# Seven Strassen products for the FFN's output projections, with operands combined by the input projections

## The chip, the cores and the metric

One core of a Trainium2 chip runs the kernel; everything is float32. The metric is the device time of one execution in microseconds. The kernel before was timed three times: 2273.18, 2268.51 and 2273.02, median 2273.02. The engines are named as in the profile: PE is the matrix engine (PEld its loading of the stationary operand), DVE the vector engine, ACT the scalar engine, POOL the third elementwise engine, SP the queue from which most transfers are issued.

## The reference

One layer of a streaming encoder on 1024 tokens of width 1024, hidden width 2816:

```python
x = x + 0.5 * swiglu_ffn(rms_norm(x, ffn1_norm), ffn1_w_in, ffn1_w_out)
u = rms_norm(x, mix_norm)
# one input projection of u; band attention A, differential attention B; gates
x = x + (g_a * (y_a @ w_branch_a) + g_b * (y_b @ w_branch_b)) @ w_o
x = x + 0.5 * swiglu_ffn(rms_norm(x, ffn2_norm), ffn2_w_in, ffn2_w_out)
return rms_norm(x, final_norm)

def swiglu_ffn(x, w_in, w_out):
    gate, up = jnp.split(x @ w_in, 2, axis=-1)
    return (silu(gate) * up) @ w_out
```

The change concerns the product with `w_out` in both FFNs: 1024 x 2816 times 2816 x 1024.

## The kernel before

**Precision.** Every float32 operand of a matmul is split into a rounded part and the remainder: `split` casts on ACT (line 95, `whi`) and subtracts on DVE (line 100, `wlo`). `mm3` (lines 124 to 128) then issues three matmuls: high x high, high x low, low x high.

**Input projections** (`ffn_in`, and the mixer's in the same way) already use seven products in place of eight, in the Winograd form of Strassen's method. `norm_pair` normalises token tile pr and token tile pr + 4 together, transposes them through PE (line 184) and stores the seven combinations `A11, A12, S1, S2, S3, S4, A22` as split pairs in fourteen buffers of the ring `big`. `weight_ops` makes `T1, T2, T3, N4` from four weight blocks, and `PRODUCTS` names the three PSUM chains q, r and s in which products are summed. For each of 22 column blocks j the seven products take 84 matmuls; the last of them is held back and issued after the first product of the next j (`later`, `flush`). The sinks apply SiLU, multiply, and store the hidden block h[j] (128 hidden channels x 1024 tokens) to device memory in two halves (line 330).

**Output projections** (`ffn_out`) are plain. The residual rows (eight tiles of 128 tokens) stay in SBUF. The hidden blocks are taken in 11 groups of two j. For a group, each hidden block and its weight rows are loaded (512 KB each) and split; then for each token tile t and each half dh of the output columns, six matmuls of 128x512 go into one bank `po`, and DVE adds half of it to the residual (line 361). In the last group the token tiles go in the order 4, 0, 5, 1, 6, 2, 7, 3, and `finish` is called behind each. In the first FFN the sums of the group before the last go to device memory and back (`x_part`), and `finish1` stores the new residual and calls `norm_pair` as soon as tiles t and t + 4 are there; `next(mix)` starts the mixer's first column block after pair 3. In the second FFN `finish2` normalises a tile and stores it. A first column block of any input projection is done in two pieces of 256 tokens, of which the first needs only pairs 0 and 1.

**Order and buffers.** The program is traced as straight code. A planner with a simulated timeline puts the instructions of each engine into a fixed order when the program is built; where an instruction is ready earlier in that simulation, it is moved ahead. At run time each engine and each queue works its list strictly in order and waits on semaphores. Buffers come from rings: `raw` (six of 4 KB for each partition), `w` (split units, 2 KB), `f` (temporaries, 2 KB), `t` (three), `big` (fourteen of 8 KB). PSUM has eight banks, six in the ring `mm` and two in `tr`.

Of the kernel before, what the change touches and what calls it, by code (L numbers as in the profile page):

```python
# [16 lines left out]
P = 128  # L17
S = 1024
# [5 lines left out]
NF = FF // P  # L24
A_HEADS, A_DIM = 8, 64
# [18 lines left out]
RAW, WU, TF, TT = 6, 20, 8, 3  # L44
# [8 lines left out]
def hybrid_layer_kernel(ctx, tc, x, ffn1_norm, ffn1_w_in, ffn1_w_out, mix_norm, w_mix_in,  # L53
# [85 lines left out]

    def rstd_row(xt):  # L140

        ssq = small.tile([P, 2], F32, tag="ssq", name="ssq")
        for d in range(2):
            nc.scalar.activation(out=junk, in_=xt[:, d * HALF:(d + 1) * HALF], func=AF.Square,
                                 scale=D ** -0.5, accum_out=ssq[:, d:d + 1])
# [20 lines left out]
    def norm_pair(pr, xt, gain, u, ps, on_vector=False):  # L166

        diag = []
        for h in range(2):
# [4 lines left out]
            for d in range(2):  # L174
                c = slice(d * HALF, (d + 1) * HALF)
                (nc.vector if on_vector else nc.gpsimd).tensor_tensor(
                    out=xt[h][:, c], in0=xt[h][:, c], in1=gain[:, c], op=ALU.mult)
        c = slice(pr * P, (pr + 1) * P)

        def block(h, d):  # L180

            tr = ps.tile([P, 4, P], F32, tag="tr", bufs=2, name="tr")
            for k in range(4):
                nc.tensor.matmul(tr[:, k, :], xt[h][:, d * HALF + k * P:d * HALF + (k + 1) * P], diag[h],  # L184
                                 start=True, stop=True)
# [125 lines left out]
    def ffn_in(w_in, u, ps, h_d, extra=None):  # L311

        silu = []
        for j in range(NF):
# [3 lines left out]
            def make_sink(c0, n, j=j):  # L318
                keep = {}

                def sink(th, blk, ap):
# [13 lines left out]
    def ffn_out(w_out, h_d, x_src, x_part, ps, finish):  # L335


        xu = [big([P, 2, D], "x", F32) for _ in range(NT // 2)]
        xs = [xu[t // 2][:, t % 2, :] for t in range(NT)]
        for t in range(NT):  # L340
            nc.scalar.dma_start(out=xs[t], in_=x_src[t])
        groups = [range(j, j + 2) for j in range(0, NF, 2)]
        for g, js in enumerate(groups):
            last = g == len(groups) - 1
            hs, ws = [], []
            for j in js:
                hr = load(h_d[j], raw_tile([P, S]))
                wr = load(w_out[j * P:(j + 1) * P, :], raw_tile([P, D]))
                hs.append([split_units(hr[:, c * HALF:(c + 1) * HALF]) for c in range(2)])
                ws.append([split_units(wr[:, c * HALF:(c + 1) * HALF]) for c in range(2)])  # L350
            for t in ([4, 0, 5, 1, 6, 2, 7, 3] if last else range(NT)):
                xt = xs[t]
                if last and x_part:
                    xt = load(x_part[t], raw_tile([P, D], "xt"))
# [517 lines left out]
```

## Time and profile before

| what | before |
|---|---|
| median of three runs | 2273.02 us |
| the profiled execution | 2272.47 us |
| its span, first to last instruction | 2270.7 us |
| busy: PE, DVE, ACT, POOL | 2160.4, 1450.3, 916.4, 286.8 us |
| mean granted clock of PE | 0.979 |
| first output projection, first to last matmul | 463 to 716 us |
| second output projection, first to last matmul | 2015 to 2261 us |

The stages in order: the first input projection to 463 us, the first output projection, the mixer's input projections and attention, the merge up to about 1600 us, the second input projection, the second output projection. A busy engine's matmuls overlap, so a matmul's listed duration is longer than its spacing. Idle time before an instruction is put down to what released it last.

### The profile page before, as it was taken

What the parts mean: (1) busy time and instruction counts of PE and PEld (TensorE: products, weight loads), DVE (VectorE), ACT (ScalarE), POOL (GpSimd) and SP (SyncE); (2) the same over time, 40 slices, a digit from 0 to 9 for tenths busy, and PEclk for the clock granted to TensorE, in tenths of its full rate; (3) what the DMA queues carried; (4) which work ended last, traced back from release to release, by engine and by line L of the source; (5) the groups of instructions that cost most, each with busy time, mean ns of one, the idle gap of its engine ahead of it and who ended that gap; (6) DMA issues with size and microseconds to landing.
All of it is one profiled execution on the core that took longest, in us unless ns stands there. A gap on an engine that the chain in (4) does not pass through costs nothing. (4 is left out here: it accounts for less than half of the span.)

```text
span 2270.7 us, 29665 instructions
## 1 busy us (share of the span) xinstructions
PE 2160.4 (95%) x10637; PEld 1827.8 (80%) x10637; DVE 1450.3 (64%) x2608; ACT 916.4 (40%) x1840; POOL 286.8 (13%) x371
## 2 busy tenths in 40 slices
PE   5999999999998899999999988899899999999998
PEld 4888888888887898888878877778788888888886
DVE  8655555566677756654378877658655555557677
ACT  5433333322124544444388755245433333322213
POOL 6021000000005100000066223004200000000000
PEclk8999999999999999999999998999899999999999
DMA  4364222433226454442596465654322222253331
GB/s 142 93 165 112 84 84 82 139 126 101 92 86 238 140 167 167 167 144 89 137 220 158 128 173 146 209 179 153 95 82 84 83 80 87 78 174 102 96 100 75
DMA packets 228611, 287.20 MB, mean 126 GB/s; under 512 B 13820, under 2 KB 160268, under 8 KB 228464
## 3 DMA queue, kind: packets, MB, share of 16 engines
q1 hardware_dynamic: 221952, 269.00, 38.9%
q0 software_dynamic: 4064, 7.39, 1.6%
q10 hardware_dynamic: 2448, 8.91, 1.1%
q8 instruction: 84, 1.38, 0.3%
q14 instruction: 63, 0.52, 0.1%
HBM read 202.14 MB, written 83.10 MB: 126 GB/s over the span
## 5 line engine op out<-in xcount | busy, mean ns | idle before, releaser
L95 ACT CAST whi<-raw 128x512 fp32r<-128x512 f32 x376 | 228.4, 622 | 664.8 <-PE po L127 321.2
L100 DVE TENSOR_TENSOR wlo<-raw,whi 128x512 fp32r<-128x512 f32 x373 | 257.1, 702 | 115.1 <-ACT whi L95 78.1
L361 DVE SCALAR_TENSOR_TENSOR x<-po,x 128x512 f32<-128x512 f32 x336 | 223.5, 687 | 119.7 <-PE po L128 119.6
L128 PE MATMUL po<-whi,wlo 128*128 128x512 f32 x704 | 273.6, 389 | 0.0
L127 PE MATMUL po<-wlo,whi 128*128 128x512 f32 x704 | 273.5, 389 | 0.0
L126 PE MATMUL po<-whi 128*128 128x512 f32 x704 | 259.6, 389 | 1.0 <-ACT whi L95 1.0
L111 DVE TENSOR_TENSOR c<-prod,c 128x512 f32<-128x512 f32 (+1 forms) x201 | 133.3, 665 | 178.9 <-PE prod L128 174.9
L100 DVE TENSOR_TENSOR wlo<-T,whi 128x512 fp32r<-128x512 f32 x189 | 134.3, 710 | 151.7 <-ACT whi L95 120.0
L95 ACT CAST whi<-T 128x512 fp32r<-128x512 f32 x192 | 120.0, 625 | 236.1 <-PE prod L127 201.2
L137 POOL TENSOR_TENSOR r<-v,neg_half 128x1 f32<-128x1 f32 x64 | 43.0, 673 | 1333.9 <-DVE v L147 1295.9
L126 PEld LDWEIGHTS po<-whi 128*128 128x128 f32 x704 | 132.0, 188 | 29.5 <-ACT whi L95 1.8
L128 PEld LDWEIGHTS po<-whi,wlo 128*128 128x128 f32 x704 | 132.1, 188 | 27.4
L127 PEld LDWEIGHTS po<-wlo,whi 128*128 128x128 f32 x704 | 132.2, 188 | 27.3
L184 PE MATMUL tr<-dg,xt 128*128 128x128 f32 x384 | 63.9, 329 | 53.2 <-DVE A22l L100 17.4
L100 DVE TENSOR_TENSOR wlo<-N,whi 128x512 fp32r<-128x512 f32 x61 | 42.2, 692 | 103.6 <-ACT whi L95 80.8
L250 ACT COPY c<-prod 128x512 f32<-128x512 f32 (+1 forms) x201 | 104.2, 574 | 5.9 <-PE prod L128 3.2
L184 PEld LDWEIGHTS tr<-dg,xt 128*128 128x128 f32 x384 | 59.2, 238 | 57.9 <-issue 25.7
L594 ACT ACTIVATE pm<-pm,mn 128x640 f32<-128x640 f32 (+7 forms) x128 | 94.1, 736 | 16.8 <-DVE mn L592 15.5
L126 PE MATMUL prod<-A11h,whi 128*128 128x512 f32 (+1 forms) x252 | 97.0, 385 | 0.9 <-ACT A11h L95 0.7
L128 PE MATMUL prod<-S1h,wlo 128*128 128x512 f32 (+1 forms) x252 | 96.1, 381 | 0.9 <-DVE wlo L100 0.9
L592 DVE CUSTOM_DVE_ANT_0 pm<-sc,nb 128x640 f32<-128x640 f32 (+7 forms) x128 | 88.1, 698 | 13.7 <-PE sc L585 10.8
L126 PE MATMUL prod<-S1h,whi 128*128 128x512 f32 (+1 forms) x252 | 96.2, 382 | 0.6 <-ACT S1h L95 0.6
(229 smaller groups left out, 5483.9 us busy)
## 6 DMA issues: line engine op xcount, KB each, us to landing
raw<-in_ffn_w_in_dram SPq DMA_DIRECT2D x88, 512.0 KB, 3.9
raw<-h SPq DMA_DIRECT2D x44, 512.0 KB, 4.0
raw<-in_ffn_w_out_dram SPq DMA_DIRECT2D x44, 512.0 KB, 4.2
h<-c SPq DMA_DIRECT2D x84, 256.0 KB, 2.0
raw<-in_w_mix_in_dram SPq DMA_DIRECT2D x40, 512.0 KB, 4.2
wr<-in_w_o_dram SPq DMA_DIRECT2D x40, 256.0 KB, 2.8
v<-vo SPq DMA_DIRECT2D x32, 256.0 KB, 2.3
qs<-q SPq DMA_DIRECT2D x16, 512.0 KB, 9.6
```

The lines of the kernel that those rows point to most:

```text
L95: nc.scalar.copy(out=hi, in_=src)
L100: (nc.gpsimd if on_pool else nc.vector).tensor_tensor(out=lo, in0=src, in1=h, op=ALU.subtract)
L111: nc.vector.tensor_tensor(out=out_, in0=a, in1=b, op=op)
L126: nc.tensor.matmul(ps, a[0], b[0], start=first, stop=False, skip_group_check=shared)
L127: nc.tensor.matmul(ps, a[0], b[1], start=False, stop=False, skip_group_check=shared)
L128: nc.tensor.matmul(ps, a[1], b[0], start=False, stop=last, skip_group_check=shared)
L137: nc.gpsimd.tensor_tensor(out=r, in0=v, in1=neg_half, op=ALU.pow)
L184: nc.tensor.matmul(tr[:, k, :], xt[h][:, d * HALF + k * P:d * HALF + (k + 1) * P], diag[h], start=True, stop=True)
L250: nc.scalar.copy(out=self.held[name], in_=p)
L361: nc.vector.scalar_tensor_tensor(out=xt[:, c], in0=po, scalar=0.5, in1=xt[:, c], op0=ALU.mult, op1=ALU.add)
L592: nc.vector.tensor_tensor_reduce(out=d3, in0=sc, in1=nb.rearrange("p (n w) -> p n w", n=n), scale=1.0, scalar=3e38, op0=ALU.add, op1=ALU.m ...
L594: nc.scalar.activation(out=dst, in_=dst, func=AF.Exp, bias=mn, scale=-1.0, accum_out=rs)
```

## The change

The output projections are done in seven products as well. The hidden matrix is divided into four: token halves (tiles 0 to 3, tiles 4 to 7) by even and odd hidden blocks; the weight matrix into even and odd hidden blocks by column halves. Each product m runs over the full contraction of one quadrant: 11 steps i, in each of which one operand block (128 channels x 512 tokens) and one weight block (128 x 512) meet, four token tiles of three matmuls each, summed in four PSUM banks over all 11 steps. The chain q holds four banks from product 0 to 6 and is read in passing after products 0, 2, 4 and 6; r (products 1 and 3) and s (product 5) share the other four. A reading adds half the banks to one quadrant of the residual.

The input projection now keeps the hidden blocks of an even and an odd j, and `hidden` forms S1, S3, S2, S4 from them on DVE and stores seven blocks for each pair of j, in place of the four halves. The weight differences are made in place in the loaded blocks, and the loads of weight blocks are placed by the table `BLOCK_LOADS`. The residual is held in halves: tokens 0 to 3 in two buffers of `big`, tiles 4 to 7 in `raw` and `f`. Quadrant (0,1) is complete after product 3, (1,1) after 4, (0,0) after 5, (1,0) after 6. The first two token groups are stored as they are complete; for the first FFN they are loaded again for `norm_pair`, which runs for all four pairs behind product 6 (`late1`), with `next(mix)` after pair 1. For the second FFN, tiles 0 to 3 are finished after product 5 (`early2`), tiles 4 to 7 at the end (`late2`). The round trip through `x_part` in the first FFN is gone. The rings change from 20 to 18 units and from 8 to 10 temporaries.

```diff
+NK = NF // 2
...
-RAW, WU, TF, TT = 6, 20, 8, 3
+RAW, WU, TF, TT = 6, 18, 10, 3
...
+    def halves(xt):
+        return [xt[:, :HALF], xt[:, HALF:]]
+    def store_rows(dst, xt):
+        for d in range(2):
+            nc.sync.dma_start(out=dst[:, d * HALF:(d + 1) * HALF], in_=xt[d])
...
                 c = slice(d * HALF, (d + 1) * HALF)
                 (nc.vector if on_vector else nc.gpsimd).tensor_tensor(
-                    out=xt[h][:, c], in0=xt[h][:, c], in1=gain[:, c], op=ALU.mult)
+                    out=xt[h][d], in0=xt[h][d], in1=gain[:, c], op=ALU.mult)
...
-    def ffn_in(w_in, u, ps, h_d, extra=None):
...
+        silu, hid = [], {}
+        def put(name, i, src):
+            nc.sync.dma_start(out=h_ops[name][i], in_=src)
+        def hidden(j, th):
+            i, odd = j // 2, j % 2
+            if (th, odd) != (1, 0):
+                put(("A11", "A22" if th else "A12")[odd], i, hid[j, th])
+            if not (odd and th):
+                return
+            a11, a21, a12, a22 = (hid.pop(k) for k in ((j - 1, 0), (j - 1, 1), (j, 0), (j, 1)))
+            s1, s2 = temp([P, HALF], "hs1"), temp([P, HALF], "hs2")
+            add(s1, a21, a22)
+            put("S1", i, s1)
+            add(a21, a11, a21, ALU.subtract)
+            put("S3", i, a21)
+            add(s2, s1, a11, ALU.subtract)
+            put("S2", i, s2)
+            add(a12, a12, s2, ALU.subtract)
+            put("S4", i, a12)
...
                     keep[th, blk] = ap
                     if (th, 0) in keep and (th, 1) in keep:
                         h = keep[th, 1]
-                        nc.vector.tensor_tensor(out=h, in0=h, in1=keep[th, 0], op=ALU.mult)
-                        nc.sync.dma_start(out=h_d[j][:, th * HALF + c0:th * HALF + c0 + n], in_=h)
+                        if n == HALF:
+                            hid[j, th] = h
+                        elif (j, th) not in hid:
+                            hid[j, th] = temp([P, HALF], "hid")
+                        nc.vector.tensor_tensor(out=h if n == HALF else hid[j, th][:, c0:c0 + n], in0=h,
+                                                in1=keep[th, 0], op=ALU.mult)
+                        if c0 + n == HALF:
+                            hidden(j, th)
                 return sink
             yield from strassen_t(weights(w_in, j * P, FF + j * P, () if j else SPARE),
                                   u, ps, make_sink, 1 if j else 2)
-    def ffn_out(w_out, h_d, x_src, x_part, ps, finish):
...
+    OUT_PRODUCTS = (("A11", "B11", "q", 0, 0, False), ("S1", "T1", "r", 1, 1, False),
+                    ("S2", "T2", "q", 0, 1, False), ("S4", "B22", "r", 0, 1, True),
+                    ("S3", "T3", "q", 1, 1, True), ("A12", "B21", "s", 0, 0, True),
+                    ("A22", "N4", "q", 1, 0, True))
...
+    BLOCK_LOADS = {(0, 0): (("B11", 0, 8),), (0, 1): (("B11", 8, 11), ("B12", 0, 4)),
+                   (0, 3): (("B12", 4, 8),), (0, 7): (("B12", 8, 11),),
+                   (1, 0): (("B22", 0, 4),), (1, 4): (("B22", 4, 8),), (1, 8): (("B22", 8, 11),),
+                   (3, 0): (("B21", 0, 4),), (3, 4): (("B21", 4, 8),), (3, 8): (("B21", 8, 11),)}
...
+    def ffn_out(w_out, x_src, x_dst, ps, early, late):
...
+        wv = w_out.rearrange("(i two p) d -> two p i d", two=2, p=P)
+        blocks, banks, begun = {}, {}, set()
+        rows = [[[None, None] for _ in range(4)] for _ in range(2)]
+        def load_block(name, i0, i1):
+            n = 2 if name == "B11" else 4
+            for j0 in range(i0, i1, n):
+                r = min(n, i1 - j0)
+                b = raw_tile([P, 2, HALF], name) if n == 2 else big([P, 4, HALF], name, F32)
+                nc.sync.dma_start(out=b[:, :r], in_=wv[int(name[1]) - 1][
+                    :, j0:j0 + r, (int(name[2]) - 1) * HALF:int(name[2]) * HALF])
+                for i in range(r):
+                    blocks[name, j0 + i] = b[:, i, :]
+        def weight(name, i):
+            if name in ("T1", "T2"):
+                t = blocks["B11", i]
+                add(t, blocks["B12" if name == "T1" else "B22", i], t, ALU.subtract)
+            elif name == "T3":
+                t = blocks["B12", i]
+                add(t, blocks["B22", i], t, ALU.subtract)
+            else:
+                t = blocks["B21" if name == "N4" else name, i]
+            return t
+        def prepare(th, dh):
+            for t in range(4):
+                if th == 0:
+                    if t % 2 == 0 and rows[0][t][1 - dh] is None:
+                        xu = big([P, 2, 2, HALF], "x", F32)
+                        for n in range(4):
+                            rows[0][t + n // 2][n % 2] = xu[:, n // 2, n % 2, :]
+                elif dh:
+                    rows[1][t][1] = temp([P, HALF], "xc")
+                elif t % 2 == 0:
+                    xu = raw_tile([P, 2, HALF], "xc")
+                    rows[1][t][0], rows[1][t + 1][0] = xu[:, 0, :], xu[:, 1, :]
+        for m, (an, bn, chain, th, dh, done) in enumerate(OUT_PRODUCTS):
+            first = chain not in banks
+            c = slice(dh * HALF, (dh + 1) * HALF)
+            if first:
+                banks[chain] = [ps.tile([P, HALF], F32, tag=tag, bufs=n, name="po") for tag, n in
+                                (("mm", 6), ("mm", 6)) + ((("mm", 6),) * 2 if chain == "q" else (("tr", 2),) * 2)]
+            for i in range(NK):
+                if (m, i) in BLOCK_LOADS:
+                    for args in BLOCK_LOADS[m, i]:
+                        load_block(*args)
+                if m:
+                    ha = temp([P, HALF], "ha")
+                else:
+                    if i % 4 == 0:
+                        h4 = big([P, 4, HALF], "ha", F32)
+                    ha = h4[:, i % 4, :]
+                a = split_units(load(h_ops[an][i], ha))
+                w = split_units(weight(bn, i))
+                if bn == "B21":
+                    n4 = blocks["B21", i]
+                    add(n4, n4, blocks["B11", i], ALU.subtract)
+                for t in range(4):
+                    mm3(banks[chain][t], [v[:, t * P:(t + 1) * P] for v in a], w,
+                        first and i == 0, i == NK - 1, not first)
+                if m == 0 and i == 0:
+                    flush()
+                if i == 5 and (th, dh) not in begun:
+                    begun.add((th, dh))
+                    prepare(th, dh)
+                    for t in range(4):
+                        load(x_src[4 * th + t][:, c], rows[th][t][dh])
+            for t in range(4):
+                xt = rows[th][t][dh]
+                nc.vector.scalar_tensor_tensor(out=xt, in0=banks[chain][t], scalar=0.5, in1=xt,
+                                               op0=ALU.mult, op1=ALU.add)
+                if done and not th:
+                    nc.sync.dma_start(out=x_dst[t][:, c], in_=xt)
+            if m == 5:
+                early()
+        late(rows[1])
...
-    h_d = drams(NF, [P, S], "h")
+    h_ops = {n: drams(NK, [P, HALF], f"h{n}") for n in U_OPS}
...
-        def finish1(t, xt):
-            if not u2:
-                u2.update(new_u())
-            nc.sync.dma_start(out=x_mid[t], in_=xt)
-            pair[t // 4] = xt
-            if t < 4:
-                norm_pair(t, [pair[0], pair[1]], gain, u2, ps)
-                if t == 3:
+        def late1(rows1):
+            for t, xt in enumerate(rows1):
+                store_rows(x_mid[4 + t], xt)
+            u2.update(new_u())
+            for t, xt in enumerate(rows1):
+                norm_pair(t, [halves(load(x_mid[t], raw_tile([P, D], "xt"))), xt], gain, u2, ps)
+                if t == 1:
                     next(mix)
...
-        ffn_out(ffn1_w_out[0], h_d, rows(x), x_part, ps, finish1)
+        ffn_out(ffn1_w_out[0], rows(x), x_mid, ps, lambda: None, late1)
...
         run_all(ffn2)
-        flush()
...
-        ffn_out(ffn2_w_out[0], h_d, x_mix, None, ps, finish2)
+        def early2():
+            for t in range(4):
+                finish2(t, halves(load(x_part[t], raw_tile([P, D], "xt"))))
+        def late2(rows1):
+            for t, xt in enumerate(rows1):
+                finish2(4 + t, xt)
+        ffn_out(ffn2_w_out[0], x_mix, x_part, ps, early2, late2)
```

More of the change, by code (lines that the diff above doesn't have):

```diff
@@ L143, in rstd_row @@
         for d in range(2):
-            nc.scalar.activation(out=junk, in_=xt[:, d * HALF:(d + 1) * HALF], func=AF.Square,
+            nc.scalar.activation(out=junk, in_=xt[d], func=AF.Square,
                                  scale=D ** -0.5, accum_out=ssq[:, d:d + 1])
@@ L183, in block @@
             for k in range(4):
-                nc.tensor.matmul(tr[:, k, :], xt[h][:, d * HALF + k * P:d * HALF + (k + 1) * P], diag[h],
+                nc.tensor.matmul(tr[:, k, :], xt[h][d][:, k * P:(k + 1) * P], diag[h],
                                  start=True, stop=True)
@@ L333, in ffn_in @@
                                   u, ps, make_sink, 1 if j else 2)
-    def ffn_out(w_out, h_d, x_src, x_part, ps, finish):
[L338 to L354, printed above, removed]
-                tc_ = slice((t % 4) * P, (t % 4 + 1) * P)
-                for dh in range(2):
-                    c = slice(dh * HALF, (dh + 1) * HALF)
-                    po = ps.tile([P, HALF], F32, tag="mm", bufs=6, name="po")
-                    for n in range(len(js)):
-                        mm3(po, [v[:, tc_] for v in hs[n][t // 4]], ws[n][dh], n == 0, n == len(js) - 1)
-                    nc.vector.scalar_tensor_tensor(out=xt[:, c], in0=po, scalar=0.5, in1=xt[:, c],
-                                                   op0=ALU.mult, op1=ALU.add)
-                if last:
-                    finish(t, xt)
-                elif x_part and g == len(groups) - 2:
-                    nc.sync.dma_start(out=x_part[t], in_=xt)
@@ L452, in hybrid_layer_kernel @@
                 gain = load_gain(ffn1_norm[0], nc.scalar)
-            norm_pair(pr, xt, gain, u, ps, pr == 0)
+            norm_pair(pr, [halves(v) for v in xt], gain, u, ps, pr == 0)
             if pr == 1:
@@ L803, in hybrid_layer_kernel @@
         u3 = {}
[L804 removed]
+        ffn2 = ffn_in(ffn2_w_in[0], u3, ps)
         for g in range(2):
@@ L823, in hybrid_layer_kernel @@
                                     u3.update(new_u())
-                                norm_pair(t, [xt[t], xt[t + 4]], gain, u3, ps)
+                                norm_pair(t, [halves(xt[t]), halves(xt[t + 4])], gain, u3, ps)
                                 if t == 3:
@@ L837, in finish2 @@
                 c = slice(d * HALF, (d + 1) * HALF)
-                nc.vector.scalar_tensor_tensor(out=o[:, c], in0=xt[:, c], scalar=r, in1=gain_f[:, c],
+                nc.vector.scalar_tensor_tensor(out=o[:, c], in0=xt[d], scalar=r, in1=gain_f[:, c],
                                                op0=ALU.mult, op1=ALU.mult)
                 nc.sync.dma_start(out=out[t * P:(t + 1) * P, c], in_=o[:, c])
-        ffn_out(ffn2_w_out[0], h_d, x_mix, None, ps, finish2)
+        def early2():
[5 more added lines that the diff above has]
+        ffn_out(ffn2_w_out[0], x_mix, x_part, ps, early2, late2)
 _INS = ['x', 'ffn1_norm', 'ffn1_w_in', 'ffn1_w_out', 'mix_norm', 'w_mix_in', 'b_gate', 'rel_bias_a',
```

7 lines of the change are left out of this document (2 added, 5 removed).

## The prediction

> **What bounds the kernel now.** I read the page first, then busy times in chosen stretches, then the groups of the first output projection alone, and last the chain and the order of time at the seams. From the page:
>
> ```profile
> span 2270.7 us, 29665 instructions
> PE 2160.4 (95%) x10637; PEld 1827.8 (80%) x10637; DVE 1450.3 (64%) x2608; ACT 916.4 (40%) x1840; POOL 286.8 (13%) x371
> L361 DVE SCALAR_TENSOR_TENSOR x<-po,x 128x512 f32<-128x512 f32 x336 | 223.5, 687 | 119.7 <-PE po L128 119.6
> L128 PE MATMUL po<-whi,wlo 128*128 128x512 f32 x704 | 273.6, 389 | 0.0
> L127 PE MATMUL po<-wlo,whi 128*128 128x512 f32 x704 | 273.5, 389 | 0.0
> L126 PE MATMUL po<-whi 128*128 128x512 f32 x704 | 259.6, 389 | 1.0 <-ACT whi L95 1.0
> ```
>
> TensorE is the busy engine, and the 3 x 704 = 2112 matmuls into `po` are the two output projections (1056 each). Their 389 ns overlap one another, so the price of one is their spacing, from the chain of waits, where each second group of 96 matmuls begins with this piece (start us, us, what):
>
> ```profile
> 2155.18 0.68 PE po L126 x3
> 2176.94 0.68 PE po L126 x3
> ```
>
> 21.76 us for 96 matmuls (2 j x 8 t x 2 dh x 3) is **0.2267 us a matmul**. Busy times by stretch (columns: length, then busy us of PE, PEld, DVE, ACT, POOL with instructions, granted clock, DMA share, GB/s):
>
> ```profile
> 250.00:440.00 190.00, 190.00 (x840) 157.30 (x839) 102.82 (x160) 68.41 (x120) 0.00 (x0) 1.00 0.26 84
> 490.00:690.00 200.00, 200.00 (x884) 165.62 (x883) 139.94 (x220) 42.15 (x72) 0.00 (x0) 1.00 0.31 100
> 716.00:760.00 44.00, 30.07 (x178) 27.09 (x177) 43.48 (x60) 26.14 (x52) 30.01 (x24) 0.81 0.44 141
> ```
>
> The first is the inside of an input projection, the second the inside of an output projection: PE has no idle time in either, at full clock, so a matmul taken out there is 0.2267 us off the end. The third is the passage from the first output projection to the mixer: there DVE is busy 43.48 of 44 us and PE waits for the normalisation.
>
> **The change part by part.** *Matmuls.* Before: 11 groups x 96 = 1056 for each projection. After: 7 products x 11 steps x 4 token tiles x 3 = 924, of the same shape (128x512 moving, 128 columns stationary), three in a row into one bank as now. 132 fewer, twice: 264 x 0.2267 = **-59.8 us**. A step (12 matmuls) then lasts 2.72 us.
>
> *What feeds a step.* Durations from the groups of the output projection alone, and from the whole run for the weight difference:
>
> ```profile
> L361 DVE SCALAR_TENSOR_TENSOR x<-po,x 128x512 f32<-128x512 f32 x148 | 98.7, 687 | 53.1 <-PE po L128 53.1
> L100 DVE TENSOR_TENSOR wlo<-raw,whi 128x512 fp32r<-128x512 f32 x72 | 47.1, 684 | 7.5 <-PE po L127 7.5
> L95 ACT CAST whi<-raw 128x512 fp32r<-128x512 f32 x72 | 42.1, 621 | 153.7 <-PE po L127 152.2
> L111 DVE TENSOR_TENSOR T<-raw 128x512 f32<-128x512 f32 x128 | 90.0, 703 | 3.9 <-DMA raw<-in_ffn_w_in_dram 2.4
> ```
>
> Splits rise from 88 to 154 for each projection (an operand and a weight block in every one of 77 steps). Weight differences are new: T1, T2, T3, N4, 11 of each, 44 DVE adds. The additions out of PSUM fall from 176 to 28, since a chain is read once after 11 steps. DVE: before 88 x 0.684 + 176 x 0.687 = 181 us of 239; after 154 x 0.684 + 44 x 0.703 + 28 x 0.687 = 155 us of 924 x 0.2267 = 209, 74%. The tightest steps (products with a difference) need 2 x 0.684 + 0.703 = 2.07 us plus 0.25 for the reads, of 2.72. ACT needs 2 x 0.621 = 1.24. So PE stays the bound, and the feed costs **0**. Its cover is the ring of units: the ACT row shows that the casts wait for PE to release units (152.2 of 153.7 us), so they run as early as the ring lets them. A ring of 18 holds 4.5 steps of four units, 12 us ahead of PE, against 0.62 + 0.68 = 1.3 us for cast and remainder. Without that cover it is 1.3 x 154 = 200 us. The ring for temporaries, 8 to 10, keeps six for operands once four hold residual halves: six steps, 16 us. I take nothing for either.
>
> *Input projection.* Each pair of j gains four DVE adds and writes seven blocks of 256 KB instead of four. 88 adds x 0.703 = 62 us over both; per 190 us (ten j) that is 14 us on DVE's 102.8, 61%, beside PE's matmuls at 100%. The transfers gain 0.79 MB per 38 us, 21 GB/s on 84. **0**; it would cost the 62 us if DVE had been the bound. The stores wait on DVE in SP's queue, with weight loads behind them; three j of raw buffers (six tiles, two each) cover that. From the DMA issues, the sequencer's own row, and the transfer rate between 440 and 480 us (each figure a 40th of it):
>
> ```profile
> h<-c SPq DMA_DIRECT2D x84, 256.0 KB, 2.0
> raw<-h SPq DMA_DIRECT2D x44, 512.0 KB, 4.0
> L117 SPq DMA_DIRECT2D raw<-h x44: 319/319/338, 399.9 to 2199.3; - x44
> GB/s 168 348 377 365 393 336 332 414 172 0 102 258 426 348 279 270 313 424 369 107 139 176 395 88 0 106 279 139 0 0 141 121 0 0 0 16 147 213 361 57
> ```
>
> *Transfers of the output projection.* 77 operand blocks (20 MB), 11.5 MB of weights, the residual rows 4 MB, now all in SP's queue: about 125 issues x 0.32 = 40 us of SP in 209, and 170 GB/s, where this row holds 332 to 414 for 6 us. The dense place is the start: in product 0's 30 us come 11 operand blocks, B11, B12 and a quarter of the rows, 2.9 + 2.9 + 2.9 + 1 = 9.7 MB. The large buffers are released from product 0 of the last j on, 16 us (six products of 2.72) before, so 46 us x 350 GB/s = 16 MB are to be had. If all had to be issued behind the stores of the last hidden block, those wait for the flushed product and its five DVE operations (2.7 + 3.5 us), and 1.75 MB of B11 and B12 (5 us) with about 1 us of split follow: 12 us for each projection. Bounds 0 and +24, I take **+2**, because PE shows no idle time at the same seam now (the row from 250 and the one from 490 frame it, and the chain has nothing there).
>
> *The passage to the mixer.* Before, the last group interleaves token tiles so that pair 0 is normalised under matmuls. After, the half (1,0) comes out of product 6 for all four pairs at the end, and the four pairs follow it. The rows around it, before (order of time), then the groups of 716 to 760, then three DVE instructions in a row and two short matmuls in a row:
>
> ```profile
> 715.71 0.39 PE L128 MATMUL po<-whi,wlo 128*128 128x512 f32 x1
> L184 PE MATMUL tr<-dg,xt 128*128 128x128 f32 x112 | 20.2, 344 | 10.9 <-DVE s L111 6.5 <-DVE A22l L100 3.1 <-ACT a L193 1.3
> L100 DVE TENSOR_TENSOR wlo<-T,whi 128x512 fp32r<-128x512 f32 x4 | 3.8, 953 | 0.0
> L176 POOL TENSOR_TENSOR xt<-xt,gain 128x512 f32<-128x512 f32 x10 | 12.9, 1324 | 0.6 <-ACT junk L144 0.6
> 743.73 0.68 DVE L100 TENSOR_TENSOR A11l<-tr,A11h 128x512 fp32r<-128x512 f32 x1
> 744.33 0.67 DVE L111 TENSOR_TENSOR s<-s,tr 128x512 f32<-128x512 f32 x1
> 744.92 0.68 DVE L111 TENSOR_TENSOR s<-tr,a 128x512 f32<-128x512 f32 x1
> 756.19 0.28 PE L126 MATMUL prod<-A11h,whi 128*128 128x256 f32 x1
> 756.31 0.28 PE L127 MATMUL prod<-A11l,whi 128*128 128x256 f32 x1
> ```
>
> Of 178 matmul records in these 44 us, 112 are transposes, 66 products of 256 columns at 0.12 us, 8 us of the mixer's work: 36 us are lost. After: DVE runs 4 reads and 4 pairs x 13 instructions (4 sums, 5 remainders, 2 diagonals, 2 small) = 56, at 43.48 / 60 = 0.725 us each 41 us, and about 4 us pass first: store of the half (2.0), because the gain overwrites it, gain (1.3), transposes and a copy. The gains and sums of the rows that are complete earlier, and the mixer's first weights, lie in product 6, where DVE is free for 12 of 30 us. Set against 45 us: the first half-width piece needs only pairs 0 and 1, 84 x 0.12 = 10 us, and A11 and S1 of the second piece another 3. Lost 32 us: **-4**. Bounds: at DVE's 0.60 spacing, 34 + 4 - 13 = 25, so -11; at the pace of the kernel's start, where four pairs also come one behind the other (below), 50 + 4 - 13 = 41, +5, and +8 with the mixer's first weights late too.
>
> ```profile
> 13.04 4.57 PE L184 MATMUL tr<-dg,xt 128*128 128x128 f32 x24 [13.04 <-DVE dg L172]
> 62.59 1.13 PE L184 MATMUL tr<-dg,xt 128*128 128x128 f32 x8 [0.88 <-DVE A22l L100]
> ```
>
> *The end.* Before:
>
> ```profile
> 2252.38 2.73 DVE L838 SCALAR_TENSOR_TENSOR o<-x,r,gain 128x512 f32<-128x512 f32 x4
> 2260.87 0.39 PE L128 MATMUL po<-whi,wlo 128*128 128x512 f32 x1
> 2265.89 1.41 DVE L838 SCALAR_TENSOR_TENSOR o<-x,r,gain 128x512 f32<-128x512 f32 x2 [0.73 <-POOL r L137]
> ```
>
> From the last matmul's end (2261.3) to the span's 2270.7 are 9.4 us, of which 3.4 follow the last output row. After, tiles 0 to 3 finish under product 6; behind the last matmul stand a read, the sum, the root and the rest of eight output halves at 0.66 us, about 7.5 us, and 3.4: **+1.5** (-1 to +4).
>
> **Sum**: -59.8 + 2 - 4 + 1.5 = -60.3 from the profiled execution's 2272.5, and 0.5 to the median: **2213 us**, its own range 2201 to 2225.
>
> **Rivals.** *Seams starve*: operands come late at the starts of both projections, +24 less the 2 counted: **2235**. For it: the stores and loads share SP's queue. Against: no such gap now.
>
> *DVE becomes the bound* in products with a difference. At the 0.953 us that a remainder took beside POOL in the passage, a step needs 3 x 0.953 + 0.25 = 3.1 us, 0.4 over, in 44 steps of each projection, 35 us: **2248**. Against: POOL is at 0.00 inside projections.
>
> *Transfers in series, slower than before.* If one waits for the one before it, products 0 and 1 (60 us of PE) need 22 operand blocks at 2.0, six tiles of B11 at 4.0, six of 1 MB (B12, B22) at 8.0 and eight half rows at 2.0: 132 us. Less 60 and the 16 us of lead, 56 us late in each projection: 2213 + 112 = **2325**. It ends behind the kernel of before from 30 us of lateness in each. Against it stands the rate row: 512 KB in 4.0 us is 131 GB/s, and the row holds 332 to 414, so several are under way at once.
>
> [...]
>
> *Not Strassen in effect* (PE's spacing gets worse with chains of 11 steps): each matmul has the shape and the order of now, and I see no row for it.
>
> **Chances.** Likeliest 0.69; starving seams 0.16; DVE the bound 0.08; series 0.05; the rest 0.02. A measurement of this kernel can't tell less than about 0.2% (4.5 us) from no change. Faster 0.93, same 0.02, slower 0.05: only the series and part of the rest end above. The range 2196 to 2238 takes in the passage's lower bound (-11, with the end's -1 and no seam: 2201, and 5 us for ten temporaries in the later stages) and the starving seams, and leaves the last three out.
>
> **What would show it.** Right: 1848 matmuls into `po`, 0.2267 us apart with PE at 100% inside both projections; DVE at some 74% there; 28 + 28 reads of PSUM; from the last `po` matmul of the first projection to a full PE some 45 us, with 256-column products in it from about 20 us on. Wrong: idle PE released by a DMA of `ha` or of weights early in a projection, by `wlo` or `T` at every step, or a passage over 50 us.

## The result, and the profile after

The changed kernel takes 2210.61 us (median of four runs, 2207.22 to 2211.25), the kernel before 2270.77 us (four runs, one more than ahead of the prediction, 2266.45 to 2273.18). The ratio is 0.9734 with a 95% interval of 0.9714 to 0.9754: 60 us faster. The prediction was 2213.

From the page of the changed kernel (busy time of each engine, then groups):

```profile
span 2209.0 us, 29778 instructions
...
PE 2100.4 (95%) x10373; PEld 1779.8 (81%) x10373; DVE 1448.2 (66%) x2620; ACT 991.2 (45%) x1972; POOL 286.4 (13%) x371
...
L128 PE MATMUL po<-wlo,whi 128*128 128x512 f32 x616 | 240.0, 390 | 0.0
...
L101 DVE TENSOR_TENSOR wlo<-B,whi 128x512 fp32r<-128x512 f32 x154 | 107.0, 695 | 129.2 <-ACT whi L96 129.2
L96 ACT CAST whi<-B 128x512 fp32r<-128x512 f32 x154 | 95.7, 622 | 206.9 <-PE po L128 185.3
```

PE has 60.0 us less busy time and the same share. 3 x 616 = 1848 matmuls go into `po`, 264 fewer. DVE does 296 additions out of PSUM fewer and 308 other instructions more (132 splits, 88 weight differences, 88 sums of hidden blocks), and its busy time stays where it was (1450.3 us before, 1448.2 now). ACT's grows by 75 us. The casts of weights still wait for PE to release units (185.3 of 206.9 us), as before.

Busy times by stretch of the changed kernel (length, then PE, PEld, DVE, ACT, POOL with instructions, granted clock, DMA share, GB/s):

```profile
250.00:440.00 190.00, 190.00 (x840) 157.43 (x839) 115.06 (x180) 69.41 (x120) 0.00 (x0) 1.00 0.32 104
457.20:686.20 229.00, 228.71 (x1008) 188.84 (x1006) 156.68 (x250) 97.67 (x175) 7.46 (x6) 1.00 0.53 173
480.00:500.00 20.00, 20.00 (x90) 16.58 (x89) 19.25 (x33) 5.68 (x10) 0.00 (x0) 1.00 0.84 298
500.00:520.00 20.00, 20.00 (x90) 16.58 (x89) 19.21 (x32) 9.78 (x17) 0.00 (x0) 1.00 0.74 255
520.00:600.00 80.00, 80.00 (x355) 66.28 (x354) 46.63 (x74) 34.16 (x60) 0.00 (x0) 1.00 0.36 107
686.20:734.90 48.70, 33.69 (x214) 31.48 (x213) 39.23 (x58) 27.55 (x62) 30.48 (x28) 0.82 0.32 101
710.00:715.00 5.00, 5.00 (x27) 5.00 (x27) 4.74 (x8) 2.08 (x4) 2.84 (x3) 0.54 0.13 44
715.00:720.00 5.00, 5.00 (x45) 5.00 (x44) 2.31 (x4) 1.04 (x3) 1.30 (x1) 1.00 0.36 105
```

Inside the input projection (first row) and the output projection (second) PE has as good as no idle time. The first output projection's stretch also holds 84 matmuls of the input projection's end: 924 + 84 = 1008. The two rows from 480 are to be remembered: DVE is busy 19.2 of 20 us there, against 46.63 of 80 behind them. The row from 686.20 is the passage to the mixer; PE does 128 transposes and 86 half-width products in its 48.7 us.

Where the 61.7 us between the two spans lie can be read from four landmarks of each kernel, the tile views of `po` and of the gates `sig` (duration min/median/max, first to last start). Before:

```profile
L128 PE MATMUL po<-whi,wlo x352: 389/389/476, 463.6 to 715.7; 128*128 128x512 f32 x176
L520 ACT ACTIVATE sig<-prod,bg x8: 682/687/690, 1018.7 to 1141.7; 128x512 f32<-128x512 f32 x8
L128 PE MATMUL po<-whi,m0l x128: 387/389/476, 1480.6 to 1575.7; 128*128 128x512 f32 x128
L128 PE MATMUL po<-whi,wlo x352: 388/389/389, 2010.5 to 2260.9; 128*128 128x512 f32 x176
```

After:

```profile
L129 PE MATMUL po<-whi,wlo x308: 388/390/390, 457.4 to 685.8; 128*128 128x512 f32 x154
L622 ACT ACTIVATE sig<-prod,bg x8: 682/682/687, 991.5 to 1114.2; 128x512 f32<-128x512 f32 x8
L129 PE MATMUL po<-whi,m0l x128: 388/390/477, 1450.3 to 1543.2; 128*128 128x512 f32 x128
L129 PE MATMUL po<-whi,wlo x308: 388/390/390, 1968.6 to 2197.0; 128*128 128x512 f32 x154
```

| stretch | before | after | difference | forecast |
|---|---|---|---|---|
| start to the last matmul of the first output projection | 715.7 | 685.8 | -29.9 | -29.9 + 1 |
| from there to the first gate (passage and mixer) | 303.0 | 305.7 | +2.7 | -4 |
| first to last gate | 123.0 | 122.7 | -0.3 | 0 |
| last gate to last matmul of the merge (attention) | 434.0 | 429.0 | -5.0 | 0 |
| from there to the last matmul of the second output projection | 685.2 | 653.8 | -31.4 | -29.9 + 1 |
| from there to the end | 9.8 | 12.0 | +2.2 | +1.5 |

So the total is right while two of its parts are not: the passage is 6.7 us worse than forecast, and 5.0 us come from the attention, where nothing was forecast. Both figures come again in other kernels: in the three of the experiments below that change neither the rings nor the passage (`cut_p5`, `dve_extra`, `dma_extra`) passage and mixer take 305.0 to 305.7 us and the attention 428.3 to 428.8.

The passage in order of time, changed kernel (start us, us, instruction, idle time before it and what ended it), PE:

```profile
685.81 0.39 PE L129 MATMUL po<-whi,wlo 128*128 128x512 f32 x1
692.23 3.79 PE L192 MATMUL tr<-dg,xc 128*128 128x128 f32 x16 [6.03 <-DVE dg L180]
...
705.99 0.38 PE L127 MATMUL prod<-A11h,whi 128*128 128x256 f32 x1 [0.68 <-ACT A11h L96]
708.57 0.58 PE L127 MATMUL prod<-S1h,whi 128*128 128x256 f32 x1 [2.19 <-ACT S1h L96]
...
733.98 1.13 PE L192 MATMUL tr<-dg,xt 128*128 128x128 f32 x8 [1.38 <-DVE A22l L101]
734.86 0.36 PE L127 MATMUL prod<-A11h,whi 128*128 128x256 f32 x1
```

The same stretch on POOL and ACT:

```profile
664.45 2.99 POOL L184 TENSOR_TENSOR xt<-xt,gain 128x512 f32<-128x512 f32 x2 [484.26 <-DMA xt<-xm]
...
686.49 2.49 POOL L184 TENSOR_TENSOR xc<-xc,gain 128x512 f32<-128x512 f32 x2
...
694.51 0.19 ACT L152 ACTIVATION_READ_ACCUMULATOR junk<-xc 128x1 f32 x1
694.60 0.56 ACT L201 COPY a<-tr 128x512 f32<-128x512 f32 x1
```

The first transposes wait 6.03 us, and the full PE comes at 734.86, 48.7 us after the last `po` matmul. Only two of the sixteen gains were done under product 6 (at 664.45); POOL did the other fourteen after 686. ACT copied pair 0's first block at 694.60, behind squares that belong to later pairs.

### The profile page after: what moved, and what is told of

It reads as the page before. It is cut to its first block, busy times and chain, and to the rows that moved or that the text cites. A ratio compares the mean times of both kernels' runs of the same rounds, so it can differ in the third digit from the quotient of the medians.

```text
span 2209.0 us, 29778 instructions
## 1 busy us (share of the span) xinstructions
PE 2100.4 (95%) x10373; PEld 1779.8 (81%) x10373; DVE 1448.2 (66%) x2620; ACT 991.2 (45%) x1972; POOL 286.4 (13%) x371
## 5 line engine op out<-in xcount | busy, mean ns | idle before, releaser
L101 DVE TENSOR_TENSOR wlo<-raw,whi 128x512 fp32r<-128x512 f32 x197 | 141.6, 719 | 183.3 <-PE prod L128 109.7
L96 ACT CAST whi<-raw 128x512 fp32r<-128x512 f32 x200 | 124.4, 622 | 273.8 <-PE prod L128 224.5
L128 PE MATMUL po<-wlo,whi 128*128 128x512 f32 x616 | 240.0, 390 | 0.0
L129 PE MATMUL po<-whi,wlo 128*128 128x512 f32 x616 | 239.9, 390 | 0.0
L101 DVE TENSOR_TENSOR wlo<-B,whi 128x512 fp32r<-128x512 f32 x154 | 107.0, 695 | 129.2 <-ACT whi L96 129.2
L96 ACT CAST whi<-B 128x512 fp32r<-128x512 f32 x154 | 95.7, 622 | 206.9 <-PE po L128 185.3
L184 POOL TENSOR_TENSOR xt<-xt,gain 128x512 f32<-128x512 f32 x36 | 49.1, 1380 | 516.4 <-DMA xt<-xm 484.3
L96 ACT CAST whi<-ha 128x512 fp32r<-128x512 f32 x154 | 94.8, 616 | 39.0 <-PE prod L128 17.2
L101 DVE TENSOR_TENSOR wlo<-ha,whi 128x512 fp32r<-128x512 f32 x154 | 105.7, 687 | 10.0 <-ACT whi L96 10.0
L127 PE MATMUL prod<-S4h,whi 128*128 128x512 f32 (+1 forms) x252 | 96.1, 381 | 1.8 <-ACT c L258 1.8
```

The source lines that it names most:

```text
L96: nc.scalar.copy(out=hi, in_=src)
L101: (nc.gpsimd if on_pool else nc.vector).tensor_tensor(out=lo, in0=src, in1=h, op=ALU.subtract)
L127: nc.tensor.matmul(ps, a[0], b[0], start=first, stop=False, skip_group_check=shared)
L128: nc.tensor.matmul(ps, a[0], b[1], start=False, stop=False, skip_group_check=shared)
L129: nc.tensor.matmul(ps, a[1], b[0], start=False, stop=last, skip_group_check=shared)
L184: (nc.vector if on_vector else nc.gpsimd).tensor_tensor(out=xt[h][d], in0=xt[h][d], in1=gain[:, c], op=ALU.mult)
```

## The experiments

All ratios are to the kernel before, timed on the same chip. Its median there was 2270.23 us beside `front_load`, `next3`, `rings_before` and `rings_after`, 2273.04 beside `front_tail`, `cut_p5`, `dve_extra` and `dma_extra`, and 2272.78 beside the two `temps8` kernels. A difference of medians to the changed kernel (measured beside 2270.77) is therefore good to some 2 us only; the places where time is won or lost are read from the landmarks of each kernel's trace. The code cuts are abridged; `...` and comments are the document's.

### The passage: order of the program or the amount of work

```diff
 # front_load: in late1, ahead of the four norm_pair calls
+for xt in rows1:                       # halves complete since product 4
+    square(xt, 1, sums[-1]); times_gain(xt, 1, gain)
+head(0); head(1)                       # load, squares, root, gains of tiles 0 and 1
...
-    norm_pair(t, [halves(load(x_mid[t], raw_tile([P, D], "xt"))), xt], gain, u2, ps)
+    norm_pair(t, [heads[t][0], xt], gain, u2, ps, ready=(heads[t][1], sums[t]))
     if t == 1:
         next(mix)
+        head(2); head(3)
```

> The changed kernel, with the passage to the mixer rewritten in its program order only: the squares and gains of the residual halves that are complete after product 4, and the loads, squares, roots and gains of tiles 0 and 1, are written ahead of everything that waits for product 6. Theory (the passage is long because ring slots and the one scratch tile of the squares are handed out in program order, so that 14 of 16 gains on POOL and 14 of 16 squares on ACT wait for product 6): 8 gains and 8 squares less behind product 6, 10 us of POOL and 6 of ACT; the first transpose some 3 us after the last matmul of product 6 instead of 6.4, S4 and S3 of the first pairs 8 to 10 us earlier, mixer 5 to 9 us earlier, 2203 to 2206. Rival (DVE's and PE's fixed order sets the passage, pairs 2 and 3 stand behind the first piece's sinks): not more than 2 us, 2209 to 2211.

Measured: 2206.41 us, 0.9718 (0.9705 to 0.9731). The interval overlaps that of the changed kernel, so the gain is read from the trace: from the last `po` matmul to the first gate 299.9 us, 5.8 less than in the changed kernel (300.2 in `front_tail`, which has the same passage). The same work stands in another order. The busy times of a stretch, of the changed kernel first:

```profile
684.00:700.00 16.00, 8.81 (x42) 7.67 (x40) 13.09 (x19) 12.15 (x33) 16.00 (x16) 0.79 0.28 99
```

and of this one:

```profile
684.00:700.00 16.00, 11.21 (x67) 9.90 (x66) 13.90 (x23) 11.06 (x27) 15.38 (x16) 0.89 0.41 136
```

PE of this one in order of time:

```profile
686.09 0.39 PE L129 MATMUL po<-whi,wlo 128*128 128x512 f32 x1
689.02 2.05 PE L212 MATMUL tr<-dg,xc 128*128 128x128 f32 x16 [2.55 <-POOL xc L204]
```

The first transposes wait 2.55 us in place of 6.03, and PE gets through 67 instructions in the 16 us where the changed kernel gets through 42. So 5.8 us of the passage were lost to work of later pairs, and of complete halves, that stood in the program behind the last half. The edit moves squares, gains, roots and loads together; what each is worth alone was not measured.

```diff
 # next3
             for t, xt in enumerate(rows1):
                 norm_pair(...)
-                if t == 1:
+                if t == 3:
                     next(mix)
```

> The changed kernel with the mixer's first piece written after pair 3 instead of pair 1, as the kernel before has it. Theory (the first piece fills the passage: 84 half-width matmuls, 10 us of PE, run while pairs 2 and 3 are normalised, only because they are written ahead of them): 5 to 10 us slower than the changed kernel, 2216 to 2221. Rival (the planner moves the piece ahead by itself, since it needs pairs 0 and 1 only): within 2 us of 2211. A result below 2209 would say that the early first piece delays pairs 2 and 3 more than it fills.

Measured: 2217.58 us, 0.9767 (0.9754 to 0.978), 7.0 us above the changed kernel; in the trace 315.5 us to the first gate, 9.8 more. That fits the prediction's price of the first half-width piece, 84 x 0.12 = 10 us: it fills time in the passage that is lost without it, and the planner does not move it ahead by itself.

### The end

```diff
 # front_tail, on top of front_load
         def late2(rows1):
+            for xt in rows1:
+                square(xt, 1, sums[-1])      # second halves, before the last read
             for t, xt in enumerate(rows1):
-                finish2(4 + t, xt)
+                finish2(4 + t, xt, sums[t])
```

> The passage rewritten as before (work that does not wait for product 6 is written ahead of it), and the same for the end: the squares of the second halves of tiles 4 to 7, complete since product 4, are written ahead of those that wait. Four squares of 0.76 us fewer stand on ACT behind the last matmul. Theory (the end, 12.0 us behind the last matmul's start against 9.8 before, is paced by ACT's eight squares): 2 us less than the version with the passage alone, 2204. Rival (DVE's eight output halves pace it, 5.3 us of work): less than 1 us.

Measured: 2203.89 us, 0.9696 (0.9681 to 0.971). Changed kernel, the end in order of time:

```profile
2195.34 2.73 DVE L463 SCALAR_TENSOR_TENSOR xc<-po,xc 128x512 f32<-128x512 f32 x4 [2.74 <-PE po L129]
2196.13 0.63 ACT L152 ACTIVATE junk<-xc 128x512 bf16<-128x512 f32 x1 [5.80 <-DVE xc L463]
...
2201.41 0.63 ACT L152 ACTIVATE junk<-xc 128x512 bf16<-128x512 f32 x1
```

The same with the second halves' squares ahead:

```profile
2189.77 0.63 ACT L175 ACTIVATE junk<-xc 128x512 bf16<-128x512 f32 x1 [2.87 <-DVE xc L483]
...
2192.03 0.63 ACT L175 ACTIVATE junk<-xc 128x512 bf16<-128x512 f32 x1
```

Eight squares from the first read on, 0.75 us apart, become four, and the stretch behind the last matmul's start falls from 12.1 (in the kernel with the new passage alone) to 9.9 us. Of the 3.0 us of squares that were moved, 2.2 came off the end; the rival, that DVE's output halves set it, had less than 1. This kernel is the fastest of the study that does the whole product, 6.7 us below the changed one.

### The matmul's price

```diff
 # cut_p5: product 5 keeps only its first step
+if m == 5 and i:
+    n4 = blocks["B21", i]
+    add(n4, n4, blocks["B11", i], ALU.subtract)
+    continue
...
-        first and i == 0, i == NK - 1, not first)
+        first and i == 0, i == NK - 1 or m == 5, not first)
```

It leaves out ten of the eleven steps by which product 5 contributes to quadrant (0,0) of the residual.

> The changed kernel with product 5 (A12 by B21) cut to the first of its 11 steps: 120 matmuls, 20 casts and 20 remainders fewer in each output projection, and ten operand loads. It leaves out most of one product's contribution to quadrant (0,0); the difference for N4 is still made. Theory (PE alone sets the projections, a step costs 12 matmuls): 2 x 120 x 0.2267 = 54.4 us less, 2156. Rival (the feed sets part of the pace, and work in later products was hidden behind product 5): clearly less than 54, since product 6 then has to wait for its eleven differences and the reload of tiles 0 to 3.

Measured: 2155.17 us, 0.9481 (0.9467 to 0.9495), 55.4 us below the changed kernel. 240 matmuls x 0.2267 is 54.4. In the trace the last matmul of the first projection starts 28.3 us earlier (1.1 of them lie ahead of the first); the stretch from the merge to the last matmul of the second is 626.3 us in place of 653.8. Half of 54.4 is 27.2. The rival, clearly less than 54 because the feed hides behind product 5, is out. Casts, remainders and loads of these steps went with the matmuls, so it is the whole step that is priced.

### What DVE has to spare

```diff
 # dve_extra: one more DVE instruction in each of the 154 steps
 w = split_units(weight(bn, i))
+nc.vector.tensor_tensor(out=w[1], in0=w[1], in1=w[1], op=ALU.max)
```

> The changed kernel with one DVE instruction of 128x512 more in each of the 154 steps (the remainder of the weight block is written once more, in place). Priced by listed durations, the steps with a difference need 3 x 0.684 + 0.703 + 0.25 = 3.0 us against PE's 2.72, 44 such steps in each projection: 25 us slower, 2236. Priced by the spacing of DVE instructions in a row (0.60), they need 2.64 and it costs nothing but its latency: 2211 to 2215. Theory: the second, since listed durations of DVE overlap as PE's do.

Measured: 2222.35 us, 0.9775 (0.9759 to 0.9791), 11.7 us more: between the two forecasts. Its stretches:

```profile
480.00:500.00 20.00, 20.00 (x90) 16.57 (x89) 20.00 (x35) 6.32 (x11) 0.00 (x0) 1.00 0.69 254
500.00:520.00 20.00, 16.24 (x65) 12.93 (x64) 20.00 (x35) 7.95 (x15) 0.00 (x0) 0.91 0.72 245
520.00:600.00 80.00, 80.00 (x355) 66.24 (x354) 64.77 (x106) 33.50 (x59) 0.00 (x0) 1.00 0.35 100
```

In the steady steps one more instruction costs nothing: from 520 to 600 DVE goes from 46.63 to 64.77 us and PE stays full. The loss is at one place, the change from product 0 to 1, where the first additions into the residual, the weight differences of T1 and the last hidden blocks meet: DVE has no idle time there for 40 us, PE is idle for 3.8, and the granted clock is 0.91. PE gets through 65 instructions in these 20 us where the changed kernel has 90; 25 x 0.2267 is 5.7 us. The last matmul of the first projection starts 4.6 us later; the second stage of this kind loses 7.0 (660.8 us from the merge in place of 653.8).

### What the transfers have to spare

```diff
 # dma_extra: each operand block of product 0 loaded twice, 2.9 MB more
 ha = h4[:, i % 4, :]
+load(h_ops[an][i], temp([P, HALF], "dm"))
```

> The changed kernel with every operand block of product 0 loaded a second time, into a temporary that nobody reads: 11 x 256 KB = 2.9 MB more in the first 30 us of each projection, ahead of the weight blocks in SP's queue. The trace of the changed kernel shows 312 GB/s and a DMA share of 0.87 from 440 to 470 us with PE at 29.71 of 30. Theory (16 us of lead cover the start, by estimate 16 MB to be had for 9.7 needed): no more than 2 us slower, 2211 to 2213. Rival (the start is at its limit): 2.9 MB at 350 GB/s is 8 us late in each projection, 2227.

Measured: 2227.36 us, 0.9797 (0.9782 to 0.9811), 16.7 us more by the medians. In the trace the first projection ends 6.4 us later and the second stage of this kind is 8.4 longer (662.2 us from the merge in place of 653.8), 14.8 together. A stretch of it:

```profile
500.00:520.00 20.00, 15.88 (x58) 12.50 (x57) 14.09 (x24) 7.06 (x13) 0.00 (x0) 0.83 0.96 342
```

Its waits from 500 to 520 (waiter, releaser, us in total, times, longest):

```profile
ACT whi L96 <- DMA ha<-hS: 13.4, 1, 13.4
...
PE po L127 <- ACT whi L96: 4.1, 1, 4.1
```

PE waits for a cast, and the casts had waited for a block of `ha`. That is the rival's size, 8 us in each projection, but not its place. The extra blocks do not spread over the start. SP worked its list in order: one was issued at 470.20 us, the other ten from 496.31 to 503.43, and product 1's first operand blocks right behind them. SP of this kernel in order of time:

```profile
496.31 1.40 SPq L118 DMA_DIRECT2D dm<-hA  x3
...
503.43 3.48 SPq L118 DMA_DIRECT2D ha<-hS  x6
```

and of the changed kernel:

```profile
497.22 1.39 SPq L118 DMA_DIRECT2D ha<-hS  x3
```

Ten blocks are 2.6 MB, 7.7 us at the 342 GB/s of the row above, and the loss is of that size. What is shown is that product 1's first operands come with little time in hand: the ten transfers put in front of them there were paid. That no transfer time is left earlier in the start is not shown; it was not tried.

### The rings

Four kernels change one line: the kernel before with 18 units and 10 temporaries or with 18 and 8, the changed one with 20 and 8 or with 18 and 8.

```diff
-RAW, WU, TF, TT = 6, 20, 8, 3
+RAW, WU, TF, TT = 6, 18, 10, 3      # rings_before; rings_after is the reverse
+RAW, WU, TF, TT = 6, 18, 8, 3       # temps8_before; temps8_after changes 18, 10 to this
```

> The kernel before with only its rings changed as the change does it: 18 split units instead of 20, 10 temporaries instead of 8. It asks where the 6.5 us came from that the stages after the mixer's input projection gained beside the Strassen products. Theory 1 (the two more temporaries let attention, the merge and its output product run ahead): about 5 us faster than before, 2266, with the stretch from the last gate activation to the last matmul of the merge some 5 us shorter. Rival (the planner happened to order those stages differently because what stands ahead of them changed): no difference beyond 2 us, or a loss from the two units fewer.

> The changed kernel with the old rings, 20 units and 8 temporaries. Theory 1 (rings): the later stages lose their 5 to 6 us again, 2216, if the output projections stand it; with four residual halves held, four temporaries are left for operands, 11 us ahead of PE, so the products themselves stay at 2.72 us a step. Rival A (planner's order): as the changed kernel, 2211 +- 2. Rival B (the products need the ten temporaries): idle PE inside the output projections, more than 2220.

> The kernel before with 18 units as in the changed kernel, but its own 8 temporaries. With 18 units and 10 temporaries its attention (from the first scores' to the last merge matmul of the earlier stage) took 428.7 us in place of 434.0, and the stretch from the last matmul of the first output projection to the first of the gates 306.2 in place of 303.0. Theory: the two more temporaries make the gain, so it is gone here: 434 us again, and the end lies within 2 us of the kernel before. Rival: the gain is not one of buffers that are free but of another fixed order, which any edit of a ring changes: then the 434 is not met again within 1.5 us, or the stretch before it moves by more than 1.5 us from both 303.0 and 306.2.

> The changed kernel with its 18 units, but 8 temporaries. Theory that the two more temporaries are what is worth something: the stretch from the last matmul of the first output projection to the first of the gates is 309 us and the attention 431, as with 20 units and 8 temporaries, and the end 5 to 6 us later than the changed kernel, 2216. Rival, that the units or the fixed order did it: 305.7 and 429 as in the changed kernel, 2210.6. Either way the output projections stay at 0.2267 us a matmul without an idle PE, 228.3 us for the first.

Measured, with the stretches of the table above (us):

| kernel | units, temporaries | median, ratio (interval) | passage and mixer | attention | last `po` to last merge matmul |
|---|---|---|---|---|---|
| before | 20, 8 | 2270.77 | 303.0 | 434.0 | 860.0 |
| temps8_before | 18, 8 | 2273.73, 1.0007 (0.9997 to 1.0017) | 305.9 | 430.1 | 858.7 |
| rings_before | 18, 10 | 2268.01, 0.999 (0.9981 to 0.9999) | 306.2 | 428.7 | 857.6 |
| rings_after | 20, 8 | 2218.21, 0.9776 (0.9758 to 0.9793) | 309.4 | 431.0 | 863.4 |
| temps8_after | 18, 8 | 2215.65, 0.9751 (0.9733 to 0.9768) | 305.0 | 428.2 | 856.0 |
| after | 18, 10 | 2210.61, 0.9734 (0.9714 to 0.9754) | 305.7 | 429.0 | 857.4 |

With 18 units the attention takes 428 to 430 us in all four kernels (and 427.6 to 428.8 in the six of the other experiments), with 20 units 431 to 434. The two more temporaries aren't the cause: beside 18 units they move it by 1.4 us one way and 0.8 the other. So the theory behind the first two runs, that the two more temporaries gain in the later stages, fell with the last two. That fewer units help the attention can't be a matter of more buffers; another fixed order is the likelier reason, but no run shows the mechanism, and it stays open. In the kernel before the same edit gives back 3 us in the passage, so over the whole stretch the rings are worth 1.3 to 2.4 us there; in the changed kernel 20 and 8 cost 6.0. What the 10 temporaries do is seen elsewhere: with 8, the changed kernel's first input projection falls behind (a stretch of temps8_after; in the changed kernel PE is busy for 50.00 us of it):

```profile
150.00:200.00 50.00, 47.69 (x204) 38.97 (x203) 28.58 (x46) 17.23 (x30) 13.19 (x34) 0.97 0.53 157
```

Its last matmul of the first output projection starts 3.2 us later, at 689.0. Its median is the 2216 of its theory, but by this route and not by the one expected; the two kernels' intervals overlap, and the trace is of the fastest of its four runs (2212.46).

## Why the prediction came out right, point by point

**The matmuls** (-59.8): right. The first stage ends 29.9 us earlier, and 132 x 0.2267 is 29.9. The agreement to the tenth is luck, since kernels with the same two stages end it anywhere from 684.8 to 686.1 us. Taking 240 matmuls out gave 55.4 us against 54.4. "Not Strassen in effect" is out.

**The feed** (0): right that PE stays the bound, with a count that is not as good as it looks. 155 us of DVE in 209 (74%) were expected, and 156.68 in 229 (68%) were found; but the 229 hold 84 matmuls of the input projection, and DVE does 250 instructions there, not the 226 that were counted, at 0.627 us of busy time each and not 0.686. The near-equal sums are luck. And the mean hid a burst: 96% from 480 to 520, 58% behind it. Of the rival *DVE becomes the bound* this much is true: there is a place where DVE is nearly the bound. It is one place, not 44 steps, and one more DVE instruction in each step is enough to make PE wait there (+11.7 us). In the steady steps the listed 0.953 us is too high a price: in the kernel with the extra instruction DVE does 106 instructions in the 80 us from 520 on, which at 0.953 would be 101 us, and PE stays full.

**The input projection** (0): right; DVE's 115.06 us in the stretch from 250 are 12.2 more, where 14 were worked out.

**The seams** (+2): the cost was 0, the lower bound, and *seams starve* did not happen. The working was too generous in two of its steps. The ring of temporaries was to keep operands "six steps, 16 us" ahead; in the changed kernel product 1's loads start at 497.22 us, by estimate 9 us ahead of its first matmul (457.0 + 216 x 0.2267 = 506.0). And "46 us x 350 GB/s = 16 MB are to be had" takes the transfers as free to move within the lead, while ten of the eleven extra blocks came to stand in front of product 1 and cost 6.4 and 8.4 us there. *Transfers in series* is out: 256 KB, 512 KB and 1 MB transfers lie over one another, as the transfer rate of the kernel with 2.9 MB more shows (each figure 1 us of the stretch from 440 to 480 us):

```profile
GB/s 88 274 385 301 168 346 246 25 2 139 350 414 358 311 395 406 377 356 410 383 393 408 391 404 410 391 344 381 340 403 406 383 326 59 0 74 279 401 295 43
```

From 450 to 473 the rate is 311 to 414 GB/s. The 35 transfers issued from 440 to 480 us took 4.1 to 6.9 us from issue to landing (medians by kind and size): one behind the other some 200 us, by estimate.

**The passage** (-4): mis-sized, +2.7. Its two steps each missed. "About 4 us pass first" was 6.03 us of idle PE, since gains and squares of complete rows did *not* lie in product 6: ring slots and scratch are handed out in the order of the program, and that work stood behind the last half. And the pace was not DVE's. 58 instructions, as counted (56), took 39.23 us, but of 48.7, so DVE itself was idle for 9.5 us, behind ACT, PE and one transfer. The first half-width product came 20.2 us behind the last `po` matmul, as forecast. Of the 48.7 us, 86 x 0.12 = 10 are products, 38 are lost where 32 were expected. The rewritten order took 5.8 of the 6.7 us back, so most of the miss is shown to be the order. Part of that may work through the clock: in the row from 710 PE is busy throughout, yet gets through 27 instructions at 0.54 where the next 5 us at 1.00 hold 45, some 2 us, and in the rewritten kernel PE has 1.00 and 45 instructions from 710 to 715. No run separates the two.

**The end** (+1.5): right in sign, +2.2 in size; the end was paced by eight squares on ACT, which the step had not counted ("a read, the sum, the root"); four fewer gave 2.2 us.

**The later stages** (0): missing from the sum. The attention gave 5.0 us and the second stage of FFN 1.5 beyond its matmuls. The range's "5 us for ten temporaries in the later stages" had the size and not the cause.

So the sum of -60.3 met -61.7 because +6.7 in the passage and -6.8 in the stages behind it (-0.3, -5.0, -1.5) cancel; the seams (-2) and the end (+0.7) make the rest. That they cancel is luck. The matmuls, 97% of the gain, are what the forecast rests on.

## What to carry to other kernels

Where PE was at 100% for whole stages, its spacing times the matmuls taken out was the gain, here to within 1.5 us a stage. Whether the feed holds is read from its densest 20 us, and from how far ahead of their use the next product's loads are issued, not from a mean over the stage or a transfer rate of another place: a stage can lose nothing and still have one place with nothing to spare. When a step was moved behind a barrier here, the order in which the program hands out its buffers decided what ran under the work ahead; putting the complete pieces first was worth 5.8 us at the passage and 2.2 at the end.

## What was unexpected of the hardware

DVE instructions whose two inputs both lie in SBUF took longer here beside POOL's 128x512 work, small ones several times as long (0.756 us against 0.155). The groups of DVE in the passage of the changed kernel (686 to 716; `tr` is in PSUM, the other inputs are in SBUF):

```profile
L155 DVE SCALAR_TENSOR_TENSOR v<-ssq 128x1 f32<-128x1 f32 x7 | 5.3, 756 | 1.7 <-ACT junk L152 1.7
...
L101 DVE TENSOR_TENSOR wlo<-raw,whi 128x512 fp32r<-128x512 f32 x2 | 3.0, 1484 | 0.0
...
L101 DVE TENSOR_TENSOR S1l<-s,S1h 128x512 fp32r<-128x512 f32 x2 | 2.2, 1122 | 0.0
...
L101 DVE TENSOR_TENSOR A11l<-tr,A11h 128x512 fp32r<-128x512 f32 x2 | 1.4, 676 | 0.0
```

DVE and POOL in order of time a little later, where POOL stands idle for 11.98 us:

```profile
726.75 0.68 DVE L101 TENSOR_TENSOR S1l<-s,S1h 128x512 fp32r<-128x512 f32 x1
...
729.96 1.27 POOL L101 TENSOR_TENSOR S3l<-s,S3h 128x512 fp32r<-128x512 f32 x1 [11.98 <-ACT S3h L96]
```

and DVE at the end (2190 to 2209), where POOL does only roots:

```profile
L155 DVE SCALAR_TENSOR_TENSOR v<-ssq 128x1 f32<-128x1 f32 x5 | 0.8, 155 | 2.0 <-ACT junk L152 2.0
```

One element for each partition took 0.756 us on average against 0.155, and a remainder 1.484 us against 0.695 over the projections. The same subtraction took 1.122 us beside POOL (`S1l`) and 0.68 without it, and where one input comes from PSUM (`A11l`) 0.676 us in the very stretch where the others are slow. No run took POOL's work away, so it is shown by the rows of one trace and not by an edit, and the reason for it is not shown.

The granted clock fell behind the idle 6.03 us: 0.57 from 690 to 695, with 16 transposes in 3.79 us where 8 took 1.13 later. Whether the idle time lowered it is not shown: the row from 710 has 0.54 again, and the longest gap of PE in the 14 us before it was 2.19 us (the line at 708.57). What lowers the clock, in either row, stays open.

```profile
690.00:695.00 5.00, 2.77 (x13) 2.77 (x14) 3.96 (x6) 4.81 (x15) 5.00 (x7) 0.57 0.00 0
```
